# Two DRAM bounces of the S5 branch issued by ScalarE, with zero blocks copied there

## The chip, the cores and the metric

The kernel runs on one core of one Trainium2 chip. The time is device microseconds of one execution, from launch to end; a time given is the median of several runs. The profile comes from one further execution. Engines are named as in the profile: PE is TensorE's matmul, PEld its weight load, DVE is VectorE, ACT is ScalarE, POOL is GpSimd, SP is SyncE, which issues DMAs.

## The reference

One layer of a decoder trunk for 512 prompt tokens and 32 sample tokens (8 sequences of 4), width 1024, float32. A normalised input is projected for four branches (Mamba-2 SSD, S5, mLSTM, cross-attention); each branch's result is projected down, weighted by a sigmoid gate and summed, and a last projection is added to the input. The part that matters here is the S5 branch: 64 groups of 16 channels, each with 64 complex states.

```python
lam_bar = jnp.exp(lam * dt)
b_bar = ((lam_bar - 1.0) / lam)[..., None] * lax.complex(b_re, b_im)
bu = jnp.einsum('gnc,btgc->btgn', b_bar, ug)
bu = bu.at[:, 0].add(lam_bar * h0)
h = jax.vmap(lambda bseq: lax.associative_scan(combine, (a_el, bseq))[1])(bu)
y = jnp.einsum('gcn,btgn->btgc', c, h).real.reshape(bsz, t, BR_WIDTH) + d_skip * u
return y, h[:, -1].real, h[:, -1].imag
```

`y` then goes through GELU and a sigmoid-gated projection.

## The kernel before

Activations lie with 128 channels on the partitions and all 544 tokens (prompt and sample) in the free dimension. Every projection is a "unit": SP loads a 128-column block of a weight matrix (`raw`, three buffers), ACT casts it to the rounded high part `whi`, DVE makes the low part `wlo`, and PE does 48 matmuls (8 blocks of K, three products of high and low parts, two token halves) into `pu`, which has two PSUM buffers. A `gate` unit is read out by ACT (`gt`, line 215), a `down` unit by DVE into `merged`.

The S5 branch works in eight blocks of 128 channels (8 groups), f = 0 to 7, called iterations. Block f needs:

- `s5_in(f)`: the projection of u, copied by ACT into the padded tile `uf` (columns for 8 shifts by 80 positions, two small blocks of it zero), written to DRAM as `ud` and read back as `U` with another layout: a transpose through DRAM.
- `s5_mats(f)` and `s5_mats2(f)`: powers of lam_bar times B and C (`bm`, `q`, `cm`, on DVE and POOL, copies on ACT), transposed by PE (`pbt`, copied to `bt`), and a local kernel `pk`, `kt`, which goes through DRAM (`kd`) to `tp`.
- `s5_scan(f)`: PE matmuls `pvr`, `pvi`, a rotation by the tables in `st` (products on DVE and POOL, `gr`, `gi`, `t`), the scan on DVE (lines 820 and 821), and copies on ACT to `hs`.
- `s5_y(f)`: matmuls `py` of `U` with `tp` and of `hs` with `cm`, copied by ACT to `yj`, written to DRAM as `yd` and read back by eight DMAs as `yt`. `yj` has the tag "uf", so it shares the one buffer of `uf`.
- `s5_out(f)`: GELU of `yt`, into `st` (lines 871 to 877).
- `s5_rot(q)`, q = 1 to 3, after iterations 0, 2 and 4: the next rotation tables, long rows of small products on POOL (`rt`, `st`). They use the two buffers of `q`.

Iteration f of the loop scans block f, makes the matrices of block f + 1, projects u for block f + 2, finishes the output of block f - 1, and multiplies out block f. Between these a generator `gd` gives gate and down units of another branch to PE, a unit for each `step`. The Tile framework sets the order of every engine's instructions from the order of the code and its own estimates, so an edit of the code moves instructions that it does not name. Each engine works its own list strictly in order, SP's included: an instruction that waits holds all behind it. All DMAs are issued by SP.

Of the kernel before, what the change touches and what calls it, by code (L numbers as in the profile page):

```python
# [16 lines left out]
P = 128  # L17
# [17 lines left out]
def hybrid_kernel(ctx: ExitStack, tc: tile.TileContext, I, O):  # L35
    nc = tc.nc
    V, G, S, T = nc.vector, nc.gpsimd, nc.scalar, nc.tensor
    dma = nc.sync.dma_start
# [6 lines left out]
    def ctile(shape, name, dt=F32):  # L45
        return cst.tile(shape, dt, name=name, tag=name)

    def bank(name="bk"):
        return pst.tile([P, 512], F32, name=name, tag="bk")

    def bc(ap, axis, n):
        ap = ap.unsqueeze(axis)
        shape = list(ap.shape)
        shape[axis] = n
        return ap.to_broadcast(shape)
# [10 lines left out]
    def stt(out, a, s, b, op0, op1):  # L66
        V.scalar_tensor_tensor(out, a, s, b, op0, op1)  # L67
# [17 lines left out]
    def wcols(c0):  # L85
        return I["w_in"][0][:, c0:c0 + P]
# [17 lines left out]
    G.memset(ones, 1.0)  # L104
    ecol = ctile([P, 1], "ecol")
    G.memset(ecol, 2.718281828459045)
    nhalf = ctile([P, 1], "nhalf")
    G.memset(nhalf, -0.5)

# [99 lines left out]
    def gate_down(k, first=False, ahead=2, place=None):  # L209
        gq = []  # L210

        def gate(i):
            pg = unit(wcols(C_G + k * D + i * P), x2)
            g = place(i) if place else ev.tile([P, NT], F32, name="gt", tag="gt")
            S.activation(halves(g), pg[:, :, 0:HALF], AF.Tanh, scale=0.5, bias=colh("b_gate", k * NK + i))  # L215
            gq.append(g)

        for i in range(ahead):
            gate(i)
            yield  # L220
        for i in range(NK):
            g = gq[i]
            pd = unit(I["w_down"][0, k][:, i * P:(i + 1) * P], o2)
            if first:
                stt(halves(merged[:, i, :]), halves(g), 1.0, pd[:, :, 0:HALF], ADD, MUL)
            else:
                stt(halves(g), halves(g), 1.0, pd[:, :, 0:HALF], ADD, MUL)
                tt(G, merged[:, i, :], merged[:, i, :], g, ADD)
            yield i + 1
            if i + ahead < NK:  # L230
                gate(i + ahead)
                yield

    def step(gen, n=1):
        for _ in range(n):
            next(gen, None)
# [104 lines left out]
    for c in range(2):  # L341
# [8 lines left out]
        for hb in range(2):  # L350
# [5 lines left out]
            f = xm0.tile([P, 4, P], F32, name="mf", tag="mf")  # L356
# [346 lines left out]
    gd = gate_down(3, first=True)  # L703
# [10 lines left out]
    def s5_in(f):  # L714
        pu = unit(wcols(C_U + f * P), x2, perm=True)
        uf = s5r.tile([P, 8, NV], F32, name="uf", tag="uf", bufs=1)
        G.memset(uf[:, 4:8, 0:8], 0.0)
        G.memset(uf[:, 0:4, 72:80], 0.0)
        S.copy(uf[:, :, 8:42], pu[:, 0, 0:272].rearrange("p (k s) -> p s k", s=8))
        S.copy(uf[:, :, 42:72], pu[:, 1, 0:240].rearrange("p (k s) -> p s k", s=8))  # L720
        us = pu[:, 1, 240:272].rearrange("p (b t) -> p t b", t=4)
        S.copy(uf[:, 0:4, 0:8], us)
        S.copy(uf[:, 4:8, 72:80], us)
        U = s5r.tile([P, 8, NV], F32, name="U", tag="U", bufs=3)
        ud = s5d.tile([8, P, NV], F32, name="ud", tag="ud")
        dma(ud.rearrange("q p k -> p q k")[:, ::-1], uf)
        dma(U, ud.rearrange("q (c g) k -> (q c) g k", g=8))

        return U
# [36 lines left out]
    def s5_mats2(f, bm, cm, bbs):  # L766
        bt = s5r.tile([P, 2, 4, P], F32, name="bt", tag="bt")
        for ri in range(2):
            pb = bank("pbt")
            for a in range(4):  # L770
                T.transpose(pb[:, a * P:(a + 1) * P], bm[:, ri, a].rearrange("p l c -> p (l c)"), ident)
            S.copy(bt[:, ri].rearrange("p a n -> p (a n)"), pb)

        pk = bank("pk")
        for g2 in range(2):
            for a in range(4):
                T.matmul(pk[32 * a:32 * a + 32, g2 * P:(g2 + 1) * P], bbs[:, a].rearrange("p g c -> p (g c)"),
                         cm[:, 2 * a + g2, 0:8, :].rearrange("p l c -> p (l c)"), start=True, stop=True,
                         tile_position=(0, 32 * a))
        kt = s5r.tile([P, 2, P], F32, name="kt", tag="kt")  # L780
        S.copy(kt.rearrange("p g x -> p (g x)"), pk[:, 0:256])
        stt(kt[:, :, 0:16], bc(i16, 1, 2), dcol[:, f:f + 1], kt[:, :, 0:16], MUL, ADD)

        kd = kds[f % 2]
        for a in range(4):
            dma(kd[:, a, :, 112:240], kt[32 * a:32 * a + 32])
        tp = [s5r.tile([P, 4, P], F32, name="tp", tag=f"tp{g2}", bufs=2) for g2 in range(2)]
        for g2 in range(2):
            dma(tp[g2], bass.AP(tensor=kd.tensor, offset=kd.offset + g2 * (16 * 1920 + 240),
                                         ap=[[16, 8], [1920, 16], [480, 4], [1, P]]))  # L790
        return bt, cm, tp, ev_[f // 2][:, :, f % 2]
# [53 lines left out]
    def s5_y(f, U, cm, tp, hs_):  # L845

        yj = s5r.tile([P, 8, 72], F32, name="yj", tag="uf")
        for hb in range(2):
            py = bank("py")
            for g4 in range(4):  # L850
                g = 4 * hb + g4
                for first, rows in ((True, U), (False, hs_)):
                    for q in range(2):
                        w = tp[g % 2][:, g // 2, 64 * q:64 * q + 64] if first else cm[:, g, 1 + 4 * q:5 + 4 * q, :].rearrange("p l c -> p (l c)")
                        T.matmul(py[64 * q:64 * q + 64, g4 * 72:(g4 + 1) * 72], w, rows[:, g, 0:72], start=first, stop=not first)
            S.copy(yj[:, 4 * hb:4 * hb + 4, :].rearrange("p g k -> p (g k)"), py[:, 0:288])
        yt = s5r.tile([P, 8, 72], F32, name="yt", tag="yt")
        yd = s5d.tile([P, 8, 72], F32, name="yd", tag="yd")
        dma(yd, yj)

        for j in range(8):
            dma(yt[:, j, :], bass.AP(tensor=yd.tensor, offset=yd.offset + j * 16 * 576, ap=[[72, 8], [576, 16], [1, 72]]))
        return yt

    def s5_out(f, yt):

        ga = stag[f]
        parts = ((yt[:, :, 8:72], ga[:, 0:TP].rearrange("p (j k) -> p j k", j=8), ga[:, 0:TP].rearrange("p (k j) -> p j k", j=8)),
                 (yt[:, 0:4, 0:8], ga[:, TP:NT].rearrange("p (t b) -> p t b", t=4), ga[:, TP:NT].rearrange("p (b t) -> p t b", t=4)))
        for y, t, _ in parts:  # L870
            S.activation(t, y, AF.Square, scale=GSQ)
            stt(t, t, 0.7978845608028654, y, ADD, MUL)
        S.activation(ga, ga, AF.Tanh)
        for y, t, _ in parts:
            stt(y, t, 1.0, y, ADD, MUL)
        for y, _, o in parts:
            S.copy(o, y)

    us_, yt = [s5_in(0)], None
    mt_ = s5_mats2(0, *s5_mats(0))  # L880
    step(gd)
    us_.append(s5_in(1))
    step(gd)
    for f in range(8):
        bt, cm, tp, E = mt_
        hs_ = s5_scan(f, us_[f], bt, E)
        if f < 7:
            ma = s5_mats(f + 1)
        step(gd)
        if f < 6:  # L890
            us_.append(s5_in(f + 2))
        if f < 7:
            mt_ = s5_mats2(f + 1, *ma)
        if f > 0:
            s5_out(f - 1, yt)
        step(gd, (0, 1, 1, 1, 1, 0, 1, 1)[f])
        yt = s5_y(f, us_[f], cm, tp, hs_)
        if f % 2 == 0 and f // 2 + 1 in range(1, 4):
            s5_rot(f // 2 + 1)
    s5_out(7, yt)  # L900

    ph = bank("pho")
    T.transpose(ph[0:64, 0:P], hp, ident)
# [2 lines left out]
    for ri in range(2):  # L906
        dma(O[6 + ri][0, 0], ho[0][0:64, 2, 64 * ri:64 * ri + 64])
        pq = bank("phq")
        for q in range(2):
            T.transpose(pq[:, q * P:(q + 1) * P], hn[:, ri].rearrange("p b a -> p (b a)")[:, q * P:(q + 1) * P], ident)  # L910
        S.copy(ho[ri][:, 0:2, :].rearrange("p q n -> p (q n)"), pq[:, 0:256])
        dma(O[13 + ri][0].rearrange("b (a h) n -> (b a) (h n)", h=2).rearrange("(q p) n -> p q n", p=P), ho[ri][:, 0:2, :])
    s5c.close()


# [28 lines left out]
    with tc.tile_pool(name="sd", bufs=1, side="right", reuse_waits="tile") as sd:  # L944
# [249 lines left out]
        gd = gate_down(1)  # L1194
# [196 lines left out]
        gd = gate_down(0)  # L1391
# [131 lines left out]
    with tc.tile_pool(name="mss", bufs=1, side="right", reuse_waits="tile") as ms:  # L1523
# [110 lines left out]
        gd = gate_down(2, ahead=8, place=lambda i: ev.tile([P, NT], F32, name="gt", tag="gt") if i < 2 else gsl[i // 2 - 1][:, i % 2])  # L1634
# [128 lines left out]
```

## Time and profile before

| | us |
|---|---|
| median of 3 runs | 1473.51 (1470.52 to 1475.09) |
| the profiled execution | 1472.34 |
| its span, first to last instruction | 1470.6 |
| PE busy in the span | 1398.0 (95%) |
| DVE, ACT, POOL busy | 858.8, 536.0, 338.9 |

The S5 loop takes the stretch from about 250 to 500 us. A timeline row gives start and length in us, engine, line, operation, out<-in and shapes, a count where equal instructions follow each other (then length and start are those of the group), and in brackets how long the engine was idle before and what ended that. "SPq" rows are the issue of a DMA by SP, not its transfer; a transfer's end is seen only where something waits for it. The granted clock is TensorE's, as a share of full speed.

### The profile page before, as it was taken

The numbers are of one execution on the slowest core, as the hardware profiler recorded it, in microseconds if no ns is written. First come the engines' busy times: TensorE is split into PE (matmuls) and PEld (weight loads), VectorE is DVE, ScalarE is ACT, GpSimd is POOL, SyncE is SP. The second block draws the span as 40 slices with busy tenths as digits, with TensorE's granted clock in tenths as the row PEclk, the third lists the DMA queues.
The fourth block names the chain that finished last, engine by engine and source line by source line (L and its number), as shares of the span: only waits on it lengthen the run. The fifth ranks groups of instructions, "written<-read, shape, count | busy, mean of one in ns | idle before, by whom it ended". The sixth has DMA issues, their size and how long they took to land. (4 is left out here: it accounts for less than half of the span.)

```text
span 1470.6 us, 28579 instructions
## 1 busy us (share of the span) xinstructions
PE 1398.0 (95%) x11713; PEld 1336.0 (91%) x11713; DVE 858.8 (58%) x1629; ACT 536.0 (36%) x953; POOL 338.9 (23%) x514
## 2 busy tenths in 40 slices
PE   6999998978879899999999999999999999899997
PEld 6998887868878899999999989999999998789997
DVE  5355496675766694677777544544343465454543
ACT  5244233444445532433333431433333332114332
POOL 3010134676483011012222222000000021110222
PEclk9999999989999999999999999999999999999999
DMA  8577362555545323333232454222222246663341
GB/s 206 166 218 234 102 198 73 120 128 117 120 106 128 102 72 90 86 80 83 62 84 74 126 168 137 64 74 72 80 73 80 73 120 180 195 201 104 101 148 62
DMA packets 298884, 172.96 MB, mean 118 GB/s; under 512 B 46749, under 2 KB 289769, under 8 KB 298754
## 3 DMA queue, kind: packets, MB, share of 16 engines
q1 hardware_dynamic: 298754, 171.14, 42.3%
q8 instruction: 92, 1.51, 0.4%
q14 instruction: 38, 0.31, 0.1%
HBM read 145.35 MB, written 25.24 MB: 116 GB/s over the span
## 5 line engine op out<-in xcount | busy, mean ns | idle before, releaser
L186 PE MATMUL pu<-xh,whi 128*128 128x272 f32 (+1 forms) x2000 | 426.4, 292 | 0.2 <-DVE hp L950 0.2
L186 PE MATMUL pu<-xl,whi 128*128 128x272 f32 (+1 forms) x2000 | 424.9, 290 | 0.5 <-DVE xl L64 0.5
L186 PE MATMUL pu<-xh,wlo 128*128 128x272 f32 (+1 forms) x2000 | 424.6, 291 | 0.0
L64 DVE TENSOR_TENSOR wlo<-raw,whi 128x1024 fp32r<-128x1024 f32 x181 | 248.6, 1373 | 228.3 <-ACT whi L175 222.8
L175 ACT CAST whi<-raw 128x1024 fp32r<-128x1024 f32 x181 | 198.7, 1098 | 453.5 <-PE pu L186 347.3
L186 PEld LDWEIGHTS pu<-xh,whi 128*128 128x128 f32 x2000 | 318.3, 189 | 5.5 <-issue 3.7
L186 PEld LDWEIGHTS pu<-xl,whi 128*128 128x128 f32 x2000 | 318.9, 190 | 4.5 <-issue 3.5
L186 PEld LDWEIGHTS pu<-xh,wlo 128*128 128x128 f32 x2000 | 317.1, 190 | 3.2 <-issue 2.9
L186 PE MATMUL pu<-oh,whi 128*128 128x272 f32 x640 | 139.6, 299 | 14.3 <-ACT gt L215 14.3
L186 PE MATMUL pu<-oh,wlo 128*128 128x272 f32 x640 | 137.4, 296 | 8.2 <-DVE wlo L64 8.2
L186 PE MATMUL pu<-ol,whi 128*128 128x272 f32 x640 | 139.1, 297 | 0.0
L186 PEld LDWEIGHTS pu<-oh,whi 128*128 128x128 f32 x640 | 105.5, 196 | 16.7 <-ACT gt L215 15.1
L186 PEld LDWEIGHTS pu<-oh,wlo 128*128 128x128 f32 x640 | 104.4, 196 | 9.1 <-DVE wlo L64 8.5
L186 PEld LDWEIGHTS pu<-ol,whi 128*128 128x128 f32 x640 | 105.6, 196 | 1.8 <-issue 1.6
L64 POOL TENSOR_TENSOR merged<-merged,gt 128x544 f32<-128x544 f32 x18 | 28.0, 1558 | 141.2 <-DVE gt L67 141.1
L67 DVE SCALAR_TENSOR_TENSOR cb<-cb,dcm,pcn 128x257 f32<-128x257 f32 x64 | 28.4, 478 | 21.3 <-PE pcn L1596 21.1
L186 PE MATMUL pu<-mh,whi 128*128 128x256 f32 x128 | 37.8, 295 | 0.1
L67 DVE SCALAR_TENSOR_TENSOR cc<-cc,dcm,pcu 128x257 f32<-128x257 f32 x24 | 11.5, 478 | 44.6 <-PE pcu L1475 44.6
L64 POOL TENSOR_TENSOR SS<-SS,dec 128x128 f32<-128x128 f32 x24 | 19.6, 815 | 77.6 <-DVE SS L1235 49.8
L186 PE MATMUL pu<-mlo,whi 128*128 128x256 f32 x128 | 37.1, 290 | 0.0
L186 PE MATMUL pu<-mh,wlo 128*128 128x256 f32 x128 | 36.2, 283 | 0.0
L1458 POOL MEMSET vtl<- 128x2 f32 x16 | 1.6, 99 | 143.3 <-PE pcu L1475 140.2
(639 smaller groups left out, 2224.7 us busy)
## 6 DMA issues: line engine op xcount, KB each, us to landing
raw<-in_w_in_dram SPq DMA_DIRECT2D x124, 512.0 KB
raw<-in_w_down_dram SPq DMA_DIRECT2D x32, 512.0 KB
kb<-in_cache_mem_k_dram SPq DMA_DIRECT2D x8, 1024.0 KB
raw<-in_w_mem_kv_dram SPq DMA_DIRECT2D x16, 512.0 KB
vb<-in_cache_mem_v_dram SPq DMA_DIRECT2D x16, 512.0 KB
cb<-in_state_mlstm_c_dram SPq DMA_DIRECT2D x16, 512.0 KB
out_dram<-cb SPq DMA_DIRECT2D x16, 512.0 KB
tp<-kd SPq DMA_DIRECT2D x16, 256.0 KB
```

Source lines behind the costliest of these rows:

```text
L64: eng.tensor_tensor(out, a, b, op)
L67: V.scalar_tensor_tensor(out, a, s, b, op0, op1)
L175: S.copy(hv, rv)
L186: T.matmul(ps[:, a, 0:c1 - c0], wt[:, k, :], xt[:, k, c0:c1], start=first, stop=last)
L1458: G.memset(vtl[:, 256:258].bitcast(F32), 0.0)
```

## The change

Five edits, all in the S5 stage:

1. The write of `uf` to `ud` and the write of `yj` to `yd` are issued by ACT in place of SP (8 each). The reads back (`U`, `yt`) stay on SP.
2. The two zero blocks of `uf` are copied by ACT from a constant tile of zeros in place of being set by POOL (16 copies of 128x32 for 16 memsets).
3. The constant tile, one more memset at the start.
4. In the loop, `step(gd, ...)`, the second of an iteration's units of `gd`, comes ahead of `s5_out(f - 1)`.
5. `s5_out(7)` comes after the end states (`hp`, `hn`) have been transposed and stored.

```diff
+    zero = ctile([P, 8], "zero")
+    G.memset(zero, 0.0)
...
-        G.memset(uf[:, 4:8, 0:8], 0.0)
-        G.memset(uf[:, 0:4, 72:80], 0.0)
+        S.copy(uf[:, 4:8, 0:8], bc(zero, 1, 4))
+        S.copy(uf[:, 0:4, 72:80], bc(zero, 1, 4))
...
-        dma(ud.rearrange("q p k -> p q k")[:, ::-1], uf)
+        nc.scalar.dma_start(ud.rearrange("q p k -> p q k")[:, ::-1], uf)
...
-        dma(yd, yj)
+        nc.scalar.dma_start(yd, yj)
...
+        step(gd, (0, 1, 1, 1, 1, 0, 1, 1)[f])
         if f > 0:
             s5_out(f - 1, yt)
-        step(gd, (0, 1, 1, 1, 1, 0, 1, 1)[f])
         yt = s5_y(f, us_[f], cm, tp, hs_)
...
-    s5_out(7, yt)
...
+    s5_out(7, yt)
     s5c.close()
```

Line numbers of the changed kernel are higher by two from the constant tile's lines on (`gt` is line 215 before and 217 now); the two zero copies of `uf` are lines 719 and 720. Three places show how instructions move. The first is ACT from the copies of `yj` of block 1 to the square of `yt` in iteration 2; before:

```order
L856 COPY yj<-py 128x288 x2
L841 COPY hs<-h_1834 64x4x8 x4
L751 COPY cm<-q_4040 64x4x144 x2
L758 COPY cm<-q_4047 64x4x144 x2
L839 COPY hs<-t_4013 64x4x64 x2
L175 CAST whi<-raw 128x1024
L871 ACTIVATE st_2893<-yt 128x32
L838 COPY hs<-t_4011 64x4x64 x2
L215 ACTIVATE gt<-pu,colH 128x544
```

and now:

```order
L728 DMA ud<-uf 128x8x80
L783 COPY kt<-pk 128x256
L177 CAST whi<-raw 128x8x8x16
L858 COPY yj<-py 128x288 x2
L843 COPY hs<-h_1836 64x4x8 x4
L753 COPY cm<-q_4042 64x4x144 x2
L861 DMA yd<-yj 128x576
L719 COPY uf<-zero 128x4x8
L720 COPY uf<-zero 128x4x8
L760 COPY cm<-q_4049 64x4x144 x2
L841 COPY hs<-t_4015 64x4x64 x2
L177 CAST whi<-raw 128x1024
```

The issue of `yd` stands between the two pairs of `cm`, with the zero copies for `uf` of block 4 behind it, and these use the buffer that `yd` reads. (`hs`, `gt` and only then the square of `yt` follow.) The `ud` at the top is that of block 3; ACT's copies of `st` from `yt` stand just ahead of it, where SP issued it as soon as `uf` was filled. On POOL the two memsets that stood between `gi` and `rt` are gone, and nothing else moves there.

The second place is ACT in iteration 3, from the `cm` pairs to the gate; before:

```order
L751 COPY cm<-q_4447 64x4x144 x2
L758 COPY cm<-q_4454 64x4x144 x2
L175 CAST whi<-raw 128x1024
L871 ACTIVATE st_2894<-yt 128x32
L839 COPY hs<-t_4420 64x4x64 x2
L215 ACTIVATE gt<-pu,colH 128x544
```

and now:

```order
L753 COPY cm<-q_4449 64x4x144 x2
L719 COPY uf<-zero 128x4x8
L720 COPY uf<-zero 128x4x8
L760 COPY cm<-q_4456 64x4x144 x2
L873 ACTIVATE st_2896<-yt 128x32
L840 COPY hs<-t_4420 64x4x64 x2
L177 CAST whi<-raw 128x1024
L217 ACTIVATE gt<-pu,colH 128x544
```

The cast `whi` for the down unit has moved from ahead of `hs` to behind it. In this iteration DVE's first scan (`gr`) moves ahead of the `q` that combines two products of POOL; before it stood behind it. Iteration 5 has both moves too.

The third place is ACT at the end of iteration 5; before:

```order
L772 COPY bt<-pbt 128x512 x2
L781 COPY kt<-pk 128x256
L856 COPY yj<-py 128x288 x2
L841 COPY hs<-h_1834 64x4x8 x4
```

and now:

```order
L774 COPY bt<-pbt 128x512 x2
L783 COPY kt<-pk 128x256
L728 DMA ud<-uf 128x8x80
L858 COPY yj<-py 128x288 x2
L843 COPY hs<-h_1836 64x4x8 x4
L753 COPY cm<-q_5514 64x4x144 x2
L861 DMA yd<-yj 128x576
```

Here `ud` of block 7 is issued behind `bt` and `kt`, and `yj`, which uses the same buffer, comes right behind it.

## The prediction

> **What bounds the kernel now.** I read the page's busy shares first, then who TensorE waits for, then stretches of the S5 stage, then its timeline. Two lines of the page:
>
> ```profile
> span 1470.6 us, 28579 instructions
> PE 1398.0 (95%) x11713; PEld 1336.0 (91%) x11713; DVE 858.8 (58%) x1629; ACT 536.0 (36%) x953; POOL 338.9 (23%) x514
> ```
>
> TensorE (PE) is the bound, so a change that adds no matmul can gain only where PE idles or runs slowly. The change touches the S5 stage alone. TensorE's waits there (245 to 520 us; total us, times, longest):
>
> ```profile
> PE pu L186 <- ACT gt L215: 14.3, 3, 5.3
> PE pu L186 <- DVE wlo L64: 8.2, 1, 8.2
> PE phq L910 <- ACT yj L856: 4.5, 1, 4.5
> PE py L855 <- ACT hs L838: 4.4, 1, 4.4
> ...
> PE py L855 <- ACT hs L839: 2.0, 1, 2.0
> ```
>
> ScalarE's `gt` holds PE three times (iterations 2, 3 and 4), its `hs` once (iteration 5). The stretches view shows that a stall costs more than itself (PE, PEld, DVE, ACT, POOL busy, then granted clock, DMA share, GB/s):
>
> ```profile
> 345.10:349.60 4.50, 0.00 (x1) 0.00 (x0) 1.86 (x4) 3.52 (x8) 4.42 (x15) 0.92 0.30 61
> 349.60:355.30 5.70, 5.67 (x25) 5.67 (x26) 3.67 (x5) 4.46 (x12) 5.70 (x12) 0.50 0.39 99
> 355.30:375.00 19.70, 19.70 (x230) 19.31 (x232) 12.90 (x21) 8.02 (x15) 14.37 (x20) 0.99 0.60 138
> ```
>
> After it PE runs 5.7 us at a clock of 0.50, which loses 5.7 x 0.5 = 2.85 us. Iteration 2 in the timeline, engine by engine (start, length):
>
> ```profile
> 329.95 0.90 ACT L856 COPY yj<-py 128x288 f32<-128x288 f32 x2
> 331.78 1.37 ACT L751 COPY cm<-q 64x576 f32<-64x576 f32 x2
> ...
> 335.73 2.59 SPq L859 DMA_DIRECT2D yd<-yj  x1
> ...
> 336.99 0.80 DVE L821 TENSOR_TENSOR_SCAN gi<-rho,gi 128x64 f32<-128x64 f32 x4
> ...
> 343.69 0.12 POOL L717 MEMSET uf<- 128x32 f32 x1 [7.32 <-DMA yd<-yj]
> ...
> 344.84 0.92 POOL L64 TENSOR_TENSOR t<-st,gi 128x256 f32<-128x256 f32 x1
> 345.72 0.57 POOL L64 TENSOR_TENSOR rt<-st,pw 128x8 f32<-128x8 f32 x2
> ...
> 344.75 0.43 DVE L64 TENSOR_TENSOR t<-t,t 128x256 f32<-128x256 f32 x1 [6.31 <-POOL t L64]
> ...
> 345.21 0.82 ACT L839 COPY hs<-t 64x256 f32<-64x256 f32 x2 [8.04 <-DVE t L64]
> 346.06 1.04 ACT L175 CAST whi<-raw 128x1024 fp32r<-128x1024 f32 x1
> ...
> 348.87 0.71 ACT L215 ACTIVATE gt<-pu,colH 128x544 f32<-128x544 f32 x1
> ...
> 349.63 0.82 PE L186 MATMUL pu<-oh,whi 128*128 128x272 f32 x2 [4.53 <-ACT gt L215]
> ```
>
> The stall starts on POOL. Its memset of `uf` waits 7.32 us for the write of `yj` (same buffer) to land, and two products `t` and the rotation tables `rt` queue behind it; VectorE, `hs`, `gt` and PE follow. Iteration 3 differs:
>
> ```profile
> 359.27 1.42 POOL L64 TENSOR_TENSOR st<-st,rt 128x256 f32<-128x256 f32 x2
> 360.73 1.58 DVE L64 TENSOR_TENSOR q<-pwi,bbr 128x512 f32<-128x512 f32 x1 [4.15 <-POOL st L64]
> 371.42 1.27 DVE L67 SCALAR_TENSOR_TENSOR q<-q,q 128x576 f32<-128x576 f32 x1 [1.23 <-POOL q L64]
> ...
> 379.14 0.82 ACT L839 COPY hs<-t 64x256 f32<-64x256 f32 x2 [0.42 <-DVE t L64]
> 379.99 0.71 ACT L215 ACTIVATE gt<-pu,colH 128x544 f32<-128x544 f32 x1
> ...
> 380.76 0.82 PE L186 MATMUL pu<-oh,whi 128*128 128x272 f32 x2 [5.25 <-ACT gt L215]
> ```
>
> There the chain begins where the rotation tables end (359.27 + 1.42 = 360.69): VectorE waits for them, and `gt` ends 20.0 us later. So the delayed tables cost a second stall. Iterations 4 and 5 repeat the pair:
>
> ```profile
> 393.15 1.36 ACT L751 COPY cm<-q 64x576 f32<-64x576 f32 x2
> 404.18 0.12 POOL L717 MEMSET uf<- 128x32 f32 x1 [6.45 <-DMA yd<-yj]
> 406.21 0.57 POOL L64 TENSOR_TENSOR rt<-st,pw 128x8 f32<-128x8 f32 x2
> ```
>
> **The change, part by part.** The rest of the prices stand in these timeline rows:
>
> ```profile
> 322.49 0.37 SPq L726 DMA_DIRECT2D ud<-uf  x1
> 326.47 1.38 ACT L877 COPY st<-yt 128x512 f32<-128x512 f32 x2 [2.25 <-DVE yt L67]
> 354.61 0.19 ACT L722 COPY uf<-pu 128x32 f32<-128x32 f32 x1
> 445.62 0.37 SPq L726 DMA_DIRECT2D ud<-uf  x1
> 447.46 0.41 ACT L781 COPY kt<-pk 128x256 f32<-128x256 f32 x1
> 448.59 0.70 ACT L856 COPY yj<-py 128x288 f32<-128x288 f32 x2 [0.71 <-DMA ud<-uf]
> 451.58 0.37 SPq L859 DMA_DIRECT2D yd<-yj  x1
> 454.67 6.07 SPq L862 DMA_DIRECT2D yt<-yd  x8
> ```
>
> How long the write of `yj` takes decides the rest. Before it took from 3.1 us (454.67 - 451.58, read back at once) to 8.0 (343.69 - 335.73, with an issue of 2.59). No row shows a DMA issued by ScalarE. I take 3.1, since on ScalarE the write comes ahead of the `tp` and weight loads that SP issued before the slow ones; 8.0 stays as the other end. The Trainium skill speaks against it: "DMA: Bandwidth & Descriptors", section "Issuing engines are not separate DMA queues", says that transfers started by different engines run on the same DMA engines and that only the issuing time is saved. By that rule the write keeps its 8.0 us and the sum below is -1.7 in place of -9.9; no run yet shows which holds.
>
> Iteration 2. The write of `uf` is now issued behind the `st<-yt` copies (326.47 + 1.38 = 327.85 in place of 322.49) and lands 2.97 us later (448.59 - 445.62), at 330.8; `yj` needs that buffer and slips 0.9 us. The first `cm` pair then ends at 334.0, where ScalarE issues `yd` (SP: 335.73). It lands at 337.1; two zero copies at 0.19 (the 128x32 row) end at 337.5, the second `cm` pair at 338.9. POOL waits for none of this: its second `t` follows the scan (336.99 + 0.80 + 0.9 = 338.7), ends at 339.6, and `rt` starts there and not at 345.72: 6.1 us earlier. `hs` starts at 340.0, and `hs`, `whi`, `hs`, `gt` (0.82 + 1.04 + 0.82 + 0.71) end at 343.4, ahead of PE's 345.1. The stall of 4.53 and the slow clock of 2.85 go. With a write of 8.0, `cm` ends at 343.7, `gt` at 347.1, and `rt` gains 2.0.
>
> Iteration 3. PE arrives 7.4 us earlier, the tables end only 6.1 earlier, so PE again waits for `gt`, some 6.5 us in place of 5.25, with the slow clock: of 7.4 us 6.1 stay. Two small shifts: the scans no longer stand behind the `q` that waited 1.23 us (gain 0 to 1.2, I take 1.2), and `whi` now stands between `hs` and `gt` (loss 0 to 1.04, I take 1.0): -0.2.
>
> Iterations 4 and 5. `cm` ends at 394.5, so `yd` is issued there and the zero copies and second `cm` end at 394.5 + 3.1 + 0.4 + 1.4 = 399.4 against `rt` at 406.21. I keep iteration 2's 6.1, since POOL's products set it, and -0.2 again. With a write of 8.0: 404.2, a gain of 2.0.
>
> Iteration 5 into 6. `ud` goes behind `kt`: 447.46 + 0.41 = 447.9 against 445.62, and `yj`, which waited for it, slips 2.25 us. `cm`, POOL's `q`, the scan, `hs` and the matmuls `py` that waited 2.0 us for `hs` slip too. I take +2.3; it is 0 if `hs` is held by something later anyway, and 4.6 if the write of `yj` slips likewise.
>
> The rest. Sixteen issues at 0.37 are 5.9 us on ScalarE: those of `yd` lie inside the landing time, those of `ud` inside the 1.7 us by which `gt` is early, except that of iteration 6: +0.4 (0 to 1.5). POOL loses sixteen memsets of 0.12, after its waits: nothing. SP no longer stops at `uf` and `yj`; its weight loads run ahead of use, which the waits of PE confirm (only `wlo`, 8.2, once, behind iteration 1's tables, which stay): nothing. `ho` ahead of `s5_out(7)` delays the last `yd` by two copies; PE's 4.5 us at `phq` is for `yj`, which comes earlier: nothing (0 to 0.9).
>
> Sum: -2 x 6.1 - 2 x 0.2 + 2.3 + 0.4 = -9.9 us. The profiled execution took 1472.34 us (1.7 beside its span), 1.2 below the median of 1473.51; so 1462.4 against it, 1463.6 against the median. I say 1463.
>
> **The rivals.** First, the wait moves to ScalarE: the write keeps 8.0 us and the zero copies hold ScalarE as the memset held POOL. For it: memset and zero copy wait for one and the same landing. Against it: the 3.1 us row, and `rt`, which is not behind the zero copies any more. -2 x 2.0 - 0.4 + 2.7 = -1.7 gives 1471, no change to be measured. The Trainium skill's rule above would have it so.
>
> Second, slower: issuing on ScalarE is dear. If an issue there takes 2.59 us as that of `yd` did on SP, and not 0.37, each `ud`, which stands ahead of `yj`, sets back `yj`, `cm`, POOL's `q` and the scan by 2.2 us in six iterations, 13.3 in all, and the write is the slow one: -1.7 + 13.3 gives 1484. It decides from 1.0 us an issue on (6.1 / 6). For it: that row. Against it: the three rows at 0.37, one of them a `yd`.
>
> Third, all four stalls go. If iterations 3 and 5 lose theirs as well, about 2 x (5.25 + 2.85) = 16 us more are gained, 1446. Against it: `gt` there hangs on tables that come only 6.1 us earlier.
>
> **Chances.** My forecast 0.64, the wait on ScalarE 0.18, dear issues 0.11, all stalls gone 0.07. The forecast's own range follows from the ends of its terms, 1457 (`whi` costing nothing, no loss at iteration 6) to 1469 (a write of 5.5 us, halfway, by which `rt` gains 4.4, and 4.6 lost at iteration 6). Leaving out most of the slower case and of the third, 8 in 10 lie in 1453 to 1475. A measurement tells about 0.3% (4.4 us) from no change. Faster is the forecast and the third rival, 0.70 without the forecast's slow end; the same is the first rival, 0.18; slower is the second and the slow end of the first, 0.12.
>
> **What would show it.** Right: no POOL wait for `yd`; `rt` about 6 us earlier after `hs`; `gt` no longer the end of a PE wait in iterations 2 and 4, with the clock at 1.00 behind them; stalls of 6 us or more left in iterations 3 and 5; ScalarE's `yj` waiting for `ud`. Wrong: zero copies waiting over 6 us for `yd`, DMA issues over 1 us on ScalarE, or a PE wait that none of these names.

## The result and the profile after

The changed kernel takes 1464.54 us (median of 9 runs, 1461.62 to 1469.82), the kernel before 1470.80 in the same rounds; the ratio is 0.9947, 95% interval 0.9932 to 0.9961. That is 5.7 to 10.0 us less, faster by more than the 0.3% that can be told from no change. The profiled execution took 1462.11 us. (Medians and ratios in this document leave out three slow executions, of 1909 to 7601 us, one each of three kernels tried below.) Two lines of its page:

```profile
span 1460.4 us, 28566 instructions
PE 1394.0 (95%) x11713; PEld 1331.1 (91%) x11713; DVE 866.4 (59%) x1629; ACT 538.2 (37%) x969; POOL 336.2 (23%) x499
```

PE does the same 11713 matmuls. TensorE's waits in the S5 stage after the change (245 to 520 us; total us, times, longest):

```profile
PE pu L188 <- ACT gt L217: 9.8, 3, 4.2
PE pk L779 <- ACT cm L760: 8.3, 5, 5.5
PE pu L188 <- DVE wlo L64: 6.3, 2, 5.7
PE py L857 <- ACT bt L774: 4.8, 2, 3.3
PE phq L911 <- ACT yj L858: 4.7, 1, 4.7
PE py L857 <- ACT hs L841: 0.8, 2, 0.6
```

The sum is 34.7 us, hardly less than the 37.6 of the same view before (the waits shown with the prediction, and two groups of 2.4 and 1.8). Some waits went, and others came. The starts of the scan's first matmuls (`pvr`) in each iteration tell where; the stage ends with the second `phq` pair. First and last row of after:

```profile
275.00 0.35 PE L802 MATMUL pvr<-U,bt 128*64 128x72 f32 x4
...
479.70 0.69 PE L911 MATMUL phq<-ident,hn 128*128 128x128 f32 x2 [4.73 <-ACT yj L858]
```

These two rows of before start at 276.31 and 486.83. From one start to the next, in us:

| iteration | 0 | 1 | 2 | 3 | 4 | 5 | 6 | 7 to phq | sum |
|---|---|---|---|---|---|---|---|---|---|
| before | 20.07 | 33.85 | 30.39 | 30.98 | 30.41 | 26.22 | 17.29 | 21.31 | 210.52 |
| after | 19.77 | 34.90 | 23.07 | 31.53 | 33.16 | 24.02 | 16.72 | 21.53 | 204.70 |
| difference | -0.30 | +1.05 | -7.32 | +0.55 | +2.75 | -2.20 | -0.57 | +0.22 | -5.82 |

This stretch is called S5 below. (The profiled spans differ by 10.2: the stage began 1.31 us earlier in the second, and 3.1 us more went behind it. Of the change only two writes of `uf` lie ahead of S5 and the last write of `yj` behind it, and the same program, profiled again below, began the stage another 2.95 us earlier. So 4.4 of the 10.2 us are not shown to be the change's.) Iteration 2 in the timeline:

```profile
331.81 0.34 ACTq L861 DMA_DIRECT2D yd<-yj  x1
336.00 0.22 ACT L719 COPY uf<-zero 128x32 f32<-128x32 f32 x1 [3.40 <-DMA yd<-yj]
338.62 0.56 POOL L64 TENSOR_TENSOR rt<-st,pw 128x8 f32<-128x8 f32 x2
339.50 0.82 ACT L841 COPY hs<-t 64x256 f32<-64x256 f32 x2 [1.76 <-DVE t L64]
342.15 0.72 ACT L217 ACTIVATE gt<-pu,colH 128x544 f32<-128x544 f32 x1
```

The write lands 336.00 - 331.81 = 4.19 us after its issue. ScalarE waits 3.40 us for it, and nobody waits for ScalarE: `rt` starts at 338.62 and `gt` ends at 342.87. PE has no wait there, and the stretch behind shows the clock at 1.00 (columns as before, granted clock ahead of the last two):

```profile
342.00:349.60 7.60, 7.60 (x74) 7.24 (x73) 3.65 (x6) 4.56 (x12) 7.60 (x16) 1.00 0.47 111
```

Iteration 4 loses time in two places:

```profile
398.05 0.23 ACT L873 ACTIVATE st<-yt 128x32 f32<-128x32 f32 x1 [3.14 <-DMA yt<-yd]
398.31 7.75 DVE L67 SCALAR_TENSOR_TENSOR st<-st,yt 128x32 f32<-128x32 f32 x1 [3.91 <-ACT st L873]
400.74 0.52 PE L188 MATMUL pu<-oh,whi 128*128 128x272 f32 x2 [1.59 <-ACT gt L217]
404.92 1.10 POOL L64 TENSOR_TENSOR q<-pwi,bbi 128x512 f32<-128x512 f32 x1
405.99 1.21 DVE L64 TENSOR_TENSOR wlo<-raw,whi 128x1024 fp32r<-128x1024 f32 x1
407.26 0.82 PE L188 MATMUL pu<-oh,wlo 128*128 128x272 f32 x2 [5.75 <-DVE wlo L64]
```

First ScalarE waits 3.14 us for `yt` (1.78 before), with `whi`, `hs` and `gt` queued behind it. Then a VectorE product of 128x32, which takes 0.18 to 0.24 us in the S5 loop of the kernel before, lasts 7.75 us. It ends at 406.06, with POOL's `q` (404.92 + 1.10 = 406.02). That `q` is the last instruction of a row that POOL works off without a gap: the products of the rotation tables (`rt`, `st`) from 393.20 on, and among the last of them two products of the matrices (`bm`, `q`). This is called POOL's row below. `wlo` stands behind the long product, and PE waits 5.75 us for `wlo`.

### The profile page after: what moved, and what is told of

Read it like the earlier page. It is cut to its first block, busy times and chain, and to the rows that moved or that the text cites. A ratio compares the mean times of both kernels' runs of the same rounds, so it can differ in the third digit from the quotient of the medians.

```text
span 1460.4 us, 28566 instructions
## 1 busy us (share of the span) xinstructions
PE 1394.0 (95%) x11713; PEld 1331.1 (91%) x11713; DVE 866.4 (59%) x1629; ACT 538.2 (37%) x969; POOL 336.2 (23%) x499
```

## The experiments

S5 is the stretch defined above, read from one profiled execution of each kernel. Its iteration 0 varies by 1.6 us between executions (a wait of 1.49 us for `bt` there comes or not), so the last column leaves iterations 0 and 1 out: from the third `pvr` to the second `phq` pair.

| kernel | median us | ratio to before, 95% | S5 | from third pvr |
|---|---|---|---|---|
| before | 1470.5 to 1472.2 | 1 | 210.52 | 156.60 |
| changed | 1464.54 | 0.9947 (0.9932 to 0.9961) | 204.70 | 150.03 |
| changed, again | 1463.66 | 0.9948 (0.9928 to 0.9968) | 205.62 | 150.99 |
| zero copies only | 1468.04 | 0.9980 (0.9966 to 0.9994) | 207.93 | 153.10 |
| ScalarE's DMAs only | 1466.40 | 0.9966 (0.9953 to 0.9979) | 205.90 | 151.88 |
| wlo ahead of st, it. 4 | 1463.45 | 0.9950 (0.9937 to 0.9964) | 205.62 | 151.01 |
| pk behind the unit, it. 1 | 1460.59 | 0.9943 (0.9923 to 0.9963) | 204.24 | 152.50 |
| tables wait for wlo, it. 4 | 1463.89 | 0.9941 (0.9919 to 0.9963) | 203.90 | 149.53 |
| gt ahead of st, it. 4 | 1461.51 | 0.9924 (0.9898 to 0.9951) | 199.64 | 144.98 |
| + gt early, it. 3 | 1458.65 | 0.9922 (0.9898 to 0.9946) | 198.83 | 144.05 |
| + pk behind the unit | 1455.64 | 0.9898 (0.9876 to 0.9921) | 196.19 | 145.08 |
| + a unit moved to it. 5 | 1457.85 | 0.9908 (0.9890 to 0.9926) | - | - |
| small early sum, it. 4 | 1464.99 | 0.9959 (0.9936 to 0.9982) | 202.08 | 149.55 |

The row "+ gt early" is built on "gt ahead of st", and each of the next two on "+ gt early". With a unit moved to iteration 5 the stretch holds 1028 recorded matmuls of units, in the other kernels 974 to 980, so its length can't be compared.

Edits 4 and 5 need no run: alone on the kernel before, they leave the order of every engine's list as it was, and taken out of the changed kernel likewise. The effect is that of edits 1 to 3.

**Zero copies only.** Edits 2 and 3 on the kernel before.

> The kernel before with the zero blocks copied by ScalarE, all DMAs still issued by SP. First theory (what counts is how soon the write of yj lands, not who sets the zero blocks): ScalarE's zero copies wait for the landing as POOL's memset did, about 6 to 7 us in iterations 2 and 4, the second cm pair and with it the rotation tables start at most 2 us earlier, and the time is 1467 to 1472, not to be told from 1470.8. Rival (the gain is that POOL no longer waits): no POOL wait for the write, rotation tables 6 us earlier, and about 1464.5 as in the changed kernel.

```profile
344.12 0.22 ACT L719 COPY uf<-zero 128x32 f32<-128x32 f32 x1 [9.22 <-DMA yd<-yj]
345.93 0.38 POOL L64 TENSOR_TENSOR rt<-st,pw 128x8 f32<-128x8 f32 x2 [4.97 <-ACT cm L760]
```

The first theory holds. The wait is ScalarE's now (9.22 us, above the 6 to 7 expected), `cm` stands behind it and the tables behind `cm`: they start 13.96 us after the third `pvr`, before 15.49, in the changed kernel 8.95. This is the prediction's first rival as a kernel of its own; the time, 1468.04, is where the first theory put it, 0.2% under the kernel before.

**ScalarE's DMAs only.** Edit 1 on the kernel before.

> The kernel before with both writes (uf and yj) issued by ScalarE, the zero blocks still set by POOL. First theory: the write of yj then lands about 4.3 us after an issue 3 us earlier, close to where POOL ends gi, POOL's memset waits under 1 us, and the time is 1463 to 1466, that of the changed kernel (1464.5). Rival (the gain is that POOL no longer waits): POOL's memset still waits 5 us or more for the write, and the time is 1468 to 1471.

```profile
335.91 0.34 ACTq L859 DMA_DIRECT2D yd<-yj  x1
338.48 0.12 POOL L717 MEMSET uf<- 128x32 f32 x1
```

The memset waits no more: the write has landed when POOL comes to it, 2.57 us after its issue. The tables start 8.97 us after the third `pvr`, as in the changed kernel, and S5 is 4.6 us shorter, of the changed kernel's 5.8. The first theory is right about the wait; the time, 1466.40, is just above its range. So the issue of the DMAs by ScalarE carries most of the gain. What the zero copies add to it, 0.9 to 1.9 us from the third `pvr` on, is little more than the 1.0 us by which the two profiles of the changed kernel differ, and the intervals of the ratios overlap.

**Place in SP's queue.** The kernel before, SP's write of `yj` put ahead of loads:

```diff
-        dma(yd, yj)
+        ydi = dma(yd, yj).ins   # in blocks 2 and 4: tp and weight loads ordered behind it
```

> The kernel before, with SP's issue of the write of yj in iterations 2 and 4 put ahead of the two tp loads and of the next weight loads. It shifts other instructions too, so only the landing of that write is read from it. First theory (the write was slow because tp and weight loads stood ahead of it in SP's queue, not because SP issued it): it lands 2.5 to 4.5 us after its issue, as it did from ScalarE (2.5 to 4.3), against 7.4 to 8.0 before. Rival (a write issued by SP is slow wherever it stands): 6 us or more.

```profile
333.28 1.28 SPq L795 DMA_DIRECT2D tp<-kd  x2
334.60 1.10 SPq L865 DMA_DIRECT2D yd<-yj  x1
340.67 0.12 POOL L721 MEMSET uf<- 128x32 f32 x1 [4.64 <-DMA yd<-yj]
...
361.08 0.55 SPq L865 DMA_DIRECT2D yd<-yj  x1
364.29 7.42 SPq L872 DMA_DIRECT2D yt<-yd  x8
...
399.87 0.34 SPq L865 DMA_DIRECT2D yd<-yj  x1
401.97 5.70 SPq L872 DMA_DIRECT2D yt<-yd  x8
```

The edit holds the writes of blocks 2 and 4 ahead of the loads. Those are issued in iterations 3 and 5; the writes behind the stalls, of blocks 1 and 3, are issued in iterations 2 and 4 and were not moved. The two that moved were read back at most 3.21 us after their issue (the middle pair, block 2) and 3.45 (block 4), where the kernel before took 5.82 and 5.77, as the first theory has it. The first rows are the write of block 1, with `tp` (two loads of 256 KB) still ahead of it: issue 1.10 us, landed after 6.07. The last pair, the write of block 3, has nothing just ahead: read back 2.10 us after issue. So SP is not slow as such; its write is slow behind the loads that it issued just before. (The one run took 1477.81 us. Much other work changed its place, so only the landings are read from it.) With a weight load of 512 KB issued by SP 0.40 us earlier, the changed kernel's write from ScalarE landed after 4.34:

```profile
385.82 0.43 SPq L82 DMA_DIRECT2D raw<-in_w_in_dram  x1
386.22 0.34 ACTq L861 DMA_DIRECT2D yd<-yj  x1
390.56 0.22 ACT L719 COPY uf<-zero 128x32 f32<-128x32 f32 x1 [3.37 <-DMA yd<-yj]
```

Before, with one such load 0.42 us ahead in SP's own queue, it took 5.82 until SP could read it back:

```profile
368.07 0.38 SPq L82 DMA_DIRECT2D raw<-in_w_in_dram  x1
368.49 0.58 SPq L859 DMA_DIRECT2D yd<-yj  x1
374.31 4.89 SPq L862 DMA_DIRECT2D yt<-yd  x8
```

In three rows each with 512 KB issued shortly ahead, then, a write from SP took 5.77 to 6.07 us and one from ScalarE 4.19 to 4.34. This hints that the issuing engine is worth about 1.5 us beside the earlier place; the rows differ in other things too, so it is not shown.

**The changed kernel again.**

> The changed kernel once more, on another chip, as the measure for the three beside it. If the 7.75 us product of iteration 4 belongs to the program and not to one execution, it lasts 7 us or more here too, and the time from the first pvr to phq is 204 to 206 us as in the first profile (204.70).

```profile
394.65 8.43 DVE L67 SCALAR_TENSOR_TENSOR st<-st,yt 128x32 f32<-128x32 f32 x1 [3.25 <-ACT st L873]
```

The product lasted 8.43 us, S5 was 205.62: it belongs to the program.

**Order of two VectorE instructions.** Iteration 4, `wlo` of the down unit ahead of the product:

```diff
+            with tc.issue_after(wlo) if f == 4 ...:   # VectorE's part of s5_out behind wlo
                 s5_out(f - 1, yt)
```

> The changed kernel with one pair of VectorE instructions exchanged, in iteration 4: wlo of the down unit ahead of the small product st<-st,yt that took 7.75 us there (0.18 us elsewhere) while POOL worked off its table products without a gap. First theory (that product is held up by POOL's unbroken row of products, and wlo and PE stand behind it): wlo runs at once in about 1.2 us, PE's wait of 5.75 us for wlo goes with the slow clock behind it (2.85 us), and iteration 5 gives back 0 to 3 us: 1456 to 1460. Rival (any product with two operands in SBUF starves beside that row): wlo itself takes 5 us or more in the place of st, PE waits as before, 1463 to 1466.

```profile
395.82 8.65 DVE L181 TENSOR_TENSOR wlo<-raw,whi 128x1024 fp32r<-128x1024 f32 x1 [4.05 <-ACT whi L180]
```

The first theory's gain did not come, and the rival is right: `wlo` takes the long duration over (8.65 us, then `st` is short). It is not the product but whatever VectorE asks for there.

**A pause in POOL's row.** In iteration 4, the first table product of 128 columns of `s5_rot` waits for `wlo`; no list changes.

```diff
+            if q == 3 and m == 4:
+                tc.add_manual_dep(first.ins, wlo, Sync ...)
```

> The changed kernel with one wait more: in iteration 4, POOL's first table product of 128 columns waits until VectorE has made wlo of the down unit. No engine's order changes. First theory (VectorE's products with two operands in SBUF cannot start while POOL works off its row without a gap, and PE waits for wlo behind them): st and wlo take 0.2 and 1.2 us, PE's wait of 5.75 us and the slow clock behind it go, the tables end 2 to 3 us later, and iteration 5, whose hs needs the tables about 20 us earlier, gets a wait of 1 to 5 us: 3 to 7 us less than the changed kernel beside it. Rival (the long duration has another cause, as a late operand of st): st or wlo still take over 5 us, nothing is gained or a microsecond lost.

```profile
395.72 0.19 DVE L67 SCALAR_TENSOR_TENSOR st<-st,yt 128x32 f32<-128x32 f32 x1 [4.59 <-ACT st L879]
396.65 1.23 DVE L182 TENSOR_TENSOR wlo<-raw,whi 128x1024 fp32r<-128x1024 f32 x1 [0.74 <-ACT whi L181]
...
428.13 0.51 PE L863 MATMUL py<-hs,cm 128*64 128x72 f32 x4 [4.40 <-ACT hs L847]
```

The cause is shown: with POOL paused, the product takes 0.19 us and `wlo` 1.23, and PE's 5.75 us are gone. The time does not move (1463.89 for 1463.66), against the 3 to 7 us expected: iteration 4 is 6.2 us shorter than in the changed kernel's second profile (26.93 for 33.17), and iterations 5 and 6 take 3.1 and 3.2 back, with waits of 4.40 and 3.61 us for `hs`.

**gt ahead of the square of yt.** Iteration 4 on ScalarE:

```diff
+            with tc.issue_after(gt) if f == 4 ...:   # ScalarE's part of s5_out behind gt
                 s5_out(f - 1, yt)
```

> The changed kernel with ScalarE's square of yt in iteration 4 put behind gt. It waited 3.14 us for the read of yt there, with whi and gt behind it. First theory: whi, hs and gt come about 3 us earlier, PE's wait of 1.59 us for gt goes, and wlo is asked for while POOL is still in its small products; if these leave VectorE room (as in iteration 2 and in the kernel before), wlo takes 1.3 us and PE's 5.75 us go as well, 5 to 8 us less than the changed kernel. Rival (POOL's row shuts VectorE out from whenever it asks): wlo starts earlier but still ends only with the row, at most 1 us gained.

```profile
395.81 1.26 DVE L181 TENSOR_TENSOR wlo<-raw,whi 128x1024 fp32r<-128x1024 f32 x1 [1.62 <-ACT whi L180]
```

The first theory holds for the waits. `wlo` comes 11.73 us after the iteration's `pvr` (395.81 - 384.08), where in the changed kernel the product ahead of it came after 14.04, and it is served; PE loses neither 1.59 nor 5.75 us. S5 is 5.1 to 6.0 us shorter than in the two profiles of the changed kernel. The time is less clear: 1461.51, 2.2 us under the changed kernel's 1463.66 of the same rounds where 5 to 8 were expected, with six runs from 1454.77 to 1463.22. In its profiled execution the parts outside S5 took 4.6 to 4.9 us longer than in the two of the changed kernel; the edit does not touch them.

**An early request.** A small sum (128x8) on VectorE, 2 us into POOL's row, ahead of the product:

```diff
+            if q == 3 and m == 2:
+                d = tt(V, dum, zero, zero, ADD)   # waits for POOL's first product of 32 columns
```

> The changed kernel with one small VectorE sum of two operands in SBUF (128x8) added in iteration 4, which waits for POOL's first table product of 32 columns, some 2 us into the row, and stands ahead of the product st that lasted 7.75 us. In the profiles so far VectorE's first request came either up to 2.9 us into the row and was served, with all later ones, or 4.5 us and more into it and waited to the row's end. First theory (an early request changes how the row runs on): the small sum takes under 0.5 us, st under 1.3 us and wlo about 1.2 us, PE's wait of 5.75 us for wlo goes; S5 199 to 203 us in place of 204.7 to 205.6. Rival (what counts is when each request comes, and from 64 columns on the row shuts VectorE out): the small sum is served, st still lasts 6 us or more, S5 as in the changed kernel.

```profile
395.45 0.19 DVE L64 TENSOR_TENSOR dum<-zero 128x8 f32<-128x8 f32 x1 [1.02 <-POOL st L64]
398.86 7.22 DVE L884 SCALAR_TENSOR_TENSOR st<-st,yt 128x32 f32<-128x32 f32 x1 [3.21 <-ACT st L883]
```

The rival is right for the product: asked for 5.6 us into the row (which starts at 393.23), it lasts 7.22 us whatever was served before. (S5 is 202.08 all the same; 1.6 of that is iteration 0.)

**pk in iteration 1.** PE's eight `pk` matmuls behind the first 18 of the down unit:

```diff
+            tc.add_manual_dep(pk[0], mm[2, lo], NoSync ...)   # iteration 1
```

> The changed kernel with the eight pk matmuls of iteration 1 moved on PE from behind the second matmul pairs of the down unit to behind its first 18 matmuls, as they stood about in the kernel before. First theory (iteration 1 lost about 1 us because pk, which waits for the last cm copies, now stands ahead of the unit that only needs wlo): PE's wait of 5.46 us for cm becomes a wait of about 3.5 us for wlo, iteration 1 loses no more than before, and the time is 1461 to 1463. Rival (the chain from the rotation tables to bt and tp sets iteration 2 whatever PE does in iteration 1): 1464 to 1465, the time moves into another wait.

```profile
315.92 0.82 PE L191 MATMUL pu<-oh,wlo 128*128 128x272 f32 x2 [2.83 <-DVE wlo L181]
349.87 0.35 PE L860 MATMUL py<-U,tp 128*64 128x72 f32 x4 [0.97 <-ACT bt L777]
```

Both are half right. Iteration 1 takes 32.00 us for 34.90, and the wait of 5.46 us for `cm` is gone; iterations 2 and 3 take 2.4 back (24.68 and 32.30 for 23.07 and 31.53).

**gt early in iteration 3**, on top of the kernel with `gt` ahead in iteration 4: `whi` and `gt` ahead of the second `cm` pair on ScalarE, `wlo` ahead of the last two `t` on VectorE.

> The kernel with gt ahead of the square in iteration 4 (1461.5, S5 stretch from first pvr to second phq 199.64), and in iteration 3 also whi and gt ahead of ScalarE's second cm pair, wlo ahead of VectorE's last two differences t, and the square of yt behind them. First theory (PE's wait of 4.16 us there comes from gt's place behind cm and hs, whose chain hangs on the tables; gt itself needs nothing of it): the wait falls under 1.5 us, the slow clock behind it goes, and 3 to 6 us are gained, less 0 to 3 us that iteration 5 gives back because hs there still waits for the tables: S5 194 to 198. Rival (the tables bound the stage whatever the order): PE waits as long at the next pk or py, S5 199 to 200.

```profile
364.30 0.71 ACT L220 ACTIVATE gt<-pu,colH 128x544 f32<-128x544 f32 x1
372.06 0.82 PE L191 MATMUL pu<-oh,wlo 128*128 128x272 f32 x2 [1.74 <-DVE wlo L181]
```

`gt` runs 9 us earlier, and PE waits 1.74 us for `wlo` in place of 4.16 for `gt`. Iteration 3 is 2.9 us shorter (28.50 for 31.43). Iterations 4 to 6 take 3.6 back, iteration 7 gives 1.5, and S5 is 0.8 shorter, 0.8 above the range expected: the first theory is right about the wait, the rival about the stage.

**With pk behind the unit as well.**

> The same with pk of iteration 1 behind 18 matmuls of the down unit. First theory: iteration 1 keeps about 2 to 3 us of gain as in the run with pk alone, of which iteration 2 and 3 give back most, since rotation tables and tp are not earlier: 0 to 1.5 us less than the kernel without it. Rival (with gt early in iteration 3 nothing there gives the gain back): 2.5 us or more less.

1455.64 us, ratio 0.9898: the lowest median of all, 15 us under the kernel before; its interval overlaps that of the kernel without this edit. From the third `pvr` on it is 1.0 us longer (145.08 for 144.05); its gain lies in iterations 0 and 1 (51.11 us for 54.78), 1.6 of it in iteration 0, which varies anyway. The 2.0 us of iteration 1 less the 1.0 given back are within the first theory's 0 to 1.5.

**A unit moved to iteration 5**, step counts (0, 1, 1, 1, 1, 1, 1, 0).

> The kernel of e9 with one down unit moved from iteration 7 to iteration 5, where PE waits 4.40 us for hs. First theory (PE waits there for want of other work, hs being bound by the tables): the unit fills the wait, PE waits under 1 us in iteration 5, but iteration 7 has a unit less ahead of phq, whose wait of 4.6 us may grow: 0 to 5 us less than the kernel of e9. Rival (the units are all needed where they stand, the wait only moves): same time within 1 us, phq or py of iteration 7 waits 4 us longer.

1457.85 us against 1458.65, with overlapping intervals: PE now waits 4.16 us for `gt` in iteration 5 and 4.55 for `hs` in iteration 7, where it waited 4.41 for `hs` in iteration 5. The wait moves, as the rival has it.

## Why the prediction was right, and where not

The time came out inside the range and on the side forecast; of 9.9 us forecast, S5 gave 5.8, the runs' interval 5.7 to 10.0. That 1464.54 lies only 1.5 us from the 1463 forecast is in part luck. The forecast was taken off a median of 1473.51; with nine runs the kernel before has 1470.80. And inside S5 the 6.9 us that iterations 4 and 5 failed to give were offset in part by 2.9 us of loss that iteration 6 did not have. One of the prediction's own signs of being wrong came as well: PE waits that it had not named, 5.75 us for `wlo` in iteration 4 and 5.46 for `cm` in iteration 1. The terms one by one:

- **Iteration 2, -7.4:** measured -7.32. The mechanism was the one named: `yd` issued from ScalarE, POOL free, `rt` 7.10 us earlier (345.72 to 338.62; counted from the iteration's `pvr` 6.5, where 6.1 was said), `gt` ended at 342.87 where 343.4 was said, no slow clock.
- **The landing time, taken at 3.1 between 3.1 and 8.0:** measured 4.19 and 4.34 where something waited for it. The difference did no harm, since `rt` was not behind the write. The rule cited against it (same DMA engines, only the issuing time saved) would have kept 8.0; the trace disagrees. The run with SP shows that a good part of those 8.0 us was what stood ahead in SP's own queue. The Trainium skill, "DMA: Bandwidth & Descriptors", section "Queues, rings and completion order", fits that better: each DMA engine takes turns between the queues that have work for it. The 4.34 against 5.82 us agrees with it; no run here holds all else equal.
- **Iteration 3, +1.1 (1.3 given back, 0.2 gained):** measured +0.55. Tables end to `gt` end is 19.98 us, where 20.0 was taken from before:

```profile
352.44 1.43 POOL L64 TENSOR_TENSOR st<-st,rt 128x256 f32<-128x256 f32 x2
373.14 0.71 ACT L217 ACTIVATE gt<-pu,colH 128x544 f32<-128x544 f32 x1
373.90 0.82 PE L188 MATMUL pu<-oh,whi 128*128 128x272 f32 x2 [4.16 <-ACT gt L217]
```

  PE's wait is 4.16 us where 6.5 was said; short waits for `wlo` and `cm`, 1.6 us together, now stand ahead of it. But "`gt` there hangs on tables" was too strong: it hangs on its place in ScalarE's list, as the run with `gt` early shows (364.30).
- **Iterations 4 and 5, -6.3:** measured +0.55. This is the step that failed: "I keep iteration 2's 6.1, since POOL's products set it". `rt` did start earlier, 8.93 us after the iteration's `pvr` (before 14.61). What was not asked is who works beside POOL's row in its new place. Before, VectorE's `st` came 2.4 us into the row and took 0.24 us (the row below); now it comes 5.1 us into it and stands to its end. The wait moved from `gt` (4.49) to `gt` and `wlo` (1.59 + 5.75). POOL gained by the same: the row took 12.8 us with VectorE shut out, where it took 16.0 before. So in iteration 5 the tables came early enough, and PE's wait for `hs` went from 4.38 to 0.24, with a wait of 3.35 for `bt` behind it (0.87 before): hence -2.20 and not a stall of 6 us, as "what would show it" had it. It fits this that the two kernels that let VectorE in again (the pause, `gt` ahead of `st`) wait 4.40 us for `hs` in iteration 5.

```profile
408.56 0.24 DVE L67 SCALAR_TENSOR_TENSOR st<-st,yt 128x32 f32<-128x32 f32 x1 [1.85 <-ACT st L871]
```

- **Iteration 6, +2.3:** measured -0.57. "`ud` goes behind `kt`" read the list as time:

```profile
438.15 0.37 ACTq L728 DMA_DIRECT2D ud<-uf  x1
439.96 0.42 ACT L783 COPY kt<-pk 128x256 f32<-128x256 f32 x1
441.08 0.40 ACT L858 COPY yj<-py 128x288 f32<-128x288 f32 x1 [0.69 <-DMA ud<-uf]
```

  `ud` was issued right behind the last copy of `uf`, 1.8 us ahead of `kt`, which stands ahead of it in ScalarE's list. `yj` waited 0.69 us, where it had waited 0.71. So the statement that each engine works its own list strictly in order holds here for ScalarE's copies, but not for the issue of a DMA among them.
- **Iteration 1, 0:** measured +1.05. The one wait of 8.2 us for `wlo`, which the forecast had staying, became two. The lists had changed here as well, and the forecast had not looked at them: on PE `pk` stood ahead of the unit's `wlo` matmuls, and on ScalarE `gt` behind `cm`.

```profile
312.31 0.82 PE L188 MATMUL pu<-oh,whi 128*128 128x272 f32 x2 [4.10 <-ACT gt L217]
319.04 1.35 PE L779 MATMUL pk<-cm,bbs 128*32 128x128 f32 x16 [5.46 <-ACT cm L760]
```

- **The rest:** ScalarE's issues took 0.33 to 0.40 us, so the second rival was wide of the mark. The first rival came true in its mechanism (zero copies waited 3.40 and 3.37 us) and not in its price. `phq` waits 4.73 for 4.51, as said.

## What to carry to other kernels

A wait on a critical chain can be taken out as forecast and a new one still appear, because the work set free runs beside other work than before: list what each engine does in the new time slot, not only what the freed engine depends on. Before a short DMA that others wait for, look at what stands ahead of it in the issuing engine's queue. And look for an instruction that stands behind a wait for something unrelated. With `gt` put ahead of the square of `yt`, S5 became shorter by about as much as by the whole change (5.1 to 6.0 us against 5.8, though the median by 2.2 only); with `gt` put early in iteration 3 as well, by 0.8 us, since the later iterations took the rest back.

## What the runs showed of the hardware beyond that

VectorE's instruction can be shut out by a whole row of POOL's, not by one instruction: 7.15 to 8.65 us in the six profiles in which it asked 4.4 to 5.7 us into the row of iteration 4, with POOL at 64 columns or more. In these the row took 12.8 us. In the other profiles of the table, and in iteration 2 of all of them, VectorE's first request behind the scan's differences `t` came 1.4 to 2.8 us into the row. It was served, and the row took 15.9 to 16.3 us: what VectorE gets, POOL pays for. (The kernel with the pause in POOL's row is left out here in iteration 4.) Later requests in such a row were served beside products of 128 columns too: with `gt` ahead in iteration 4, `wlo` got in at 395.81 and then `st` in 0.20 us. The small sum, served as early, did not have that effect. What decides when VectorE gets its turn stays open. The Trainium skill, "SBUF — State Buffer", section "SBUF: two separate sides", has the two engines share a pair of ports, held for a whole instruction; the trace agrees that one stands while the other works, but the page speaks of one instruction, and here VectorE stood for more than ten.
